# Row sums on one core: the first buffer filled by one load instead of two, and sixteen short reads issued by GpSimd

## The chip, the core and the metric

The kernel runs on one core of a Trainium2 chip. The metric is the device time of the run in microseconds (us). Before the change it is 162.26 us, the median of four runs (162.17 to 162.42).

## What is computed

The input is 32 x 512 rows of 1,024 float32 numbers, 64 MiB; the output is the sum of each row, 16,384 numbers.

```python
def reference(x):                  # x: (32, 512, 1024) float32
    return np.sum(x, axis=-1).astype(np.float32)
```

## The kernel before

The 16,384 rows are spread over 128 partitions, 128 rows on each. `BLOCKS` cuts these 128 into two blocks of 112 and 16 rows per partition; within a block a partition holds rows that follow each other in memory. A block is worked in buffers of `G` = 16 rows per partition, 8,192 KB each: seven for the first block and one for the second. Three such buffers exist (`xpool`, `bufs=3`), so the load into a buffer waits until the reduce of the buffer three before it is done.

All loads are issued by SyncE (`nc.sync.dma_start`, L81, and L95 and L98 for the last buffer). The first buffer is filled by two loads, row 0 of each partition (512 KB) and rows 1 to 15 (7,680 KB); `parts` in L79 says so. The others of the first block take one load each. The last buffer is loaded in five pieces of falling size (9, 4 and 2 rows, then 544 and 480 columns of the last row), so that little work is left behind the last byte.

VectorE sums most rows with one `tensor_reduce` per buffer (L43). ScalarE takes 7 rows of the seventh buffer and some of the last, with an activation that accumulates (L51). The last rows go through a paired add on VectorE (L59), with a one-column copy (L112) between two of them. ScalarE issues the first block's output (L89), SyncE the second's (L114), which is the last transfer.

The order around the change comes from three places. A tile framework puts instructions on each engine's queue in the order in which the program names them, and adds the semaphore waits that the data need. At the very end SyncE waits for every semaphore of the kernel. And after compilation L124 to L143 move the first `EARLY` = 2 instructions of SyncE's body, which are the two loads of the first buffer, ahead of the barrier with which the kernel starts:

```python
loads = [i for i in code if i.engine == sp][:EARLY]
...
at = next(k for k, i in enumerate(code) if i.engine == sp and i.opcode == "Drain")
code[at:at] = loads
```

GpSimd does nothing but set four constants at the start and take part in the barriers.

Of the kernel before, what the change touches and what calls it, by code (L numbers as in the profile page):

```python
# [1 line left out]

# [4 lines left out]

F32 = mybir.dt.float32
ADD = mybir.AluOpType.add
COPY = mybir.ActivationFunctionType.Copy  # L10
X = mybir.AxisListType.X

BLOCKS = (112, 16)
G = 16
ACT_ROWS = 7
CUT = 544
EARLY = 2


@with_exitstack  # L20
def row_sums(
    ctx: ExitStack,
    tc: tile.TileContext,
    x: bass.AP,
    out: bass.AP,
):
    nc = tc.nc
    P = nc.NUM_PARTITIONS

    x_flat = x.flatten_outer_dims()  # L30
    R, D = x_flat.shape
    C = R // P
    assert R % P == 0 and sum(BLOCKS) == C
    out_flat = out.rearrange("a (b c) -> (a b c)", c=1)

    xpool = ctx.enter_context(tc.tile_pool(name="x", bufs=3))
    rpool = ctx.enter_context(tc.tile_pool(name="res", bufs=1))
    part = rpool.tile([P, 1], F32, name="part")
    seen = rpool.tile([P, 1], F32, name="seen")
    pairs = [rpool.tile([P, D // 2], F32, name=f"pairs{i}") for i in range(3)]  # L40

    def rows_dve(xt, res, j, n, c):
        nc.vector.tensor_reduce(  # L43
            out=res[:, c : c + n],
            in_=xt[:, j * D : (j + n) * D].rearrange("p (j d) -> p j d", d=D),
            axis=X,
            op=ADD,
        )

    def sum_act(v, acc):  # L50
        nc.scalar.activation(out=v, in_=v, func=COPY, accum_out=acc)  # L51

    def rows_act(xt, res, j, n, c):
        for i in range(n):
            sum_act(xt[:, (j + i) * D : (j + i + 1) * D], res[:, c + i : c + i + 1])

    def pairs_dve(xt, a, b, first, acc, pairs):
        h = (a + b) // 2
        nc.vector.tensor_tensor_reduce(  # L59
            out=pairs[:, 0 : h - a], in0=xt[:, a:h], in1=xt[:, h:b], scale=1.0, scalar=first,  # L60
            op0=ADD, op1=ADD, accum_out=acc,
        )

    def block(r0, n):
        x_b = x_flat[r0 : r0 + P * n].rearrange("(p c) d -> p (c d)", p=P)
        out_b = out_flat[r0 : r0 + P * n].rearrange("(p c) -> p c", p=P)
        return x_b, out_b, rpool.tile([P, n], F32, name=f"res{r0}")

    full = C - G
    done = 0  # L70
    for b, n in enumerate(BLOCKS):
        x_b, out_b, res = block(done * P, n)
        final = b == len(BLOCKS) - 1
        whole = n - G if final else n
        c = 0
        while c < whole:
            m = min(G, whole - c)
            xt = xpool.tile([P, G * D], F32, tag="xt", name="xt")
            parts = (0, 1, m) if done + c == 0 else (0, m)  # L79
            for i, k in zip(parts, parts[1:]):  # L80
                nc.sync.dma_start(  # L81
                    out=xt[:, i * D : k * D], in_=x_b[:, (c + i) * D : (c + k) * D]
                )
            a = ACT_ROWS if done + c + m == full else 0
            rows_dve(xt, res, 0, m - a, c)
            rows_act(xt, res, m - a, a, c + m - a)
            c += m
        if not final:
            nc.scalar.dma_start(out=out_b, in_=res)  # L89
        done += n  # L90

    xt = xpool.tile([P, G * D], F32, tag="xt", name="xt")
    cuts = [0, 9, 13, 15]
    for i, k in zip(cuts, cuts[1:]):
        nc.sync.dma_start(out=xt[:, i * D : k * D], in_=x_b[:, (c + i) * D : (c + k) * D])  # L95
    last = 15 * D
    for i, k in ((0, CUT), (CUT, D)):
        nc.sync.dma_start(  # L98
            out=xt[:, last + i : last + k],
            in_=x_b[:, c * D + last + i : c * D + last + k],  # L100
        )

    for i, k in zip(cuts[:2], cuts[1:3]):
        h = (k - i) // 2
        rows_dve(xt, res, i, h, c + i)
        rows_act(xt, res, i + h, k - i - h, c + i + h)
    pairs_dve(xt, 13 * D, 14 * D, 0.0, res[:, c + 13 : c + 14], pairs[2])
    rows_act(xt, res, 14, 1, c + 14)
    pairs_dve(xt, last, last + CUT, 0.0, part, pairs[0])


    nc.vector.tensor_copy(out=seen, in_=part)  # L112
    pairs_dve(xt, last + CUT, last + D, part, res[:, c + 15 : c + 16], pairs[1])
    nc.sync.dma_start(out=out_b, in_=res)  # L114


def kernel(tc: tile.TileContext, x: bass.AP, out: bass.AP):
    row_sums(tc, x, out)
    tc.close()
    tc.compile()  # L120

    sp = mybir.EngineType.SP  # L124
    fn = tc.nc.m.functions[0]
    entry, body = None, None
    for blk in fn.blocks:
        ops = [i for i in blk.instructions if i.engine == sp]
        if entry is None:
            entry = blk  # L130
        elif any(i.opcode == "DMACopy" for i in ops):
            body = blk
            break
    code = list(body.instructions)
    loads = [i for i in code if i.engine == sp][:EARLY]
    for load in loads:
        assert load.opcode == "DMACopy" and not load.sync_info.on_wait
        code.remove(load)
    body.instructions = code
    code = list(entry.instructions)  # L140
    at = next(k for k, i in enumerate(code) if i.engine == sp and i.opcode == "Drain")
    code[at:at] = loads
    entry.instructions = code  # L143

# [1 line left out]
_INS = ['x']  # L146
_OUTS = [((32, 512), 'float32')]


# [23 lines left out]
```

## Time and profile before

| what | value |
|---|---|
| median of four runs | 162.26 us |
| the profiled execution's own time | 162.35 us |
| its span, first to last instruction | 160.6 us |
| reduce of a whole buffer (L43, 128x16384) | 17.22 us |
| starts of the first four reduces | 21.84, 41.12, 60.47, 79.82 us |
| HBM read over the span | 67.11 MB, 418 GB/s with what is written |
| from issue to landing: load of 512 KB | 3.6 us |
| from issue to landing: load of 7,680 KB | 21.3 us |
| from issue to landing: output from ScalarE's queue, 56 KB | 7.5 us |
| from issue to landing: output from SyncE's queue, 8 KB | 1.4 us |

The page gives for each engine the time in which it computed; issuing a transfer is not counted as busy. DMA queues are listed by packets: a packet is one contiguous row moved by one of the core's 16 DMA engines, or the four bytes with which an engine reports its share of a transfer as done. q1 is SyncE's queue and q10 ScalarE's. A row of the waits says which engine waited, at which line, for what, and then the us in total, the number of times and the longest. In a table of stretches, a packet is counted where it starts, so short stretches can show a DMA share over 1.

### The profile page before, as it was taken

To read this page: it belongs to the slowest core of one execution; us is meant where nothing else is said; L and a number is where in the kernel's file an instruction comes from. 1 tells how busy PE (TensorE), PEld (TensorE's weight loads), DVE (VectorE), ACT (ScalarE), POOL (GpSimd) and SP (SyncE) were. 2 spreads that over 40 slices of the span, in tenths; PEclk is the share of its full clock that TensorE was granted. 3 is DMA by queue.
4 is the path that set the end of the run, shared out by engine and by line. 5 is a ranking of instruction groups with operands and counts; after the bars stand their busy time and mean duration, and the time that the engine had idled before them with its cause. 6 is when DMAs were issued, how large, how long until landed. Compare 5 with 4: busy or idle time off the path is not lost.

```text
span 160.6 us, 119 instructions
## 1 busy us (share of the span) xinstructions
DVE 121.5 (76%) x16; ACT 17.2 (11%) x31; POOL 0.2 (0%) x4
## 2 busy tenths in 40 slices
DVE  0000059997799959999499994999949998697884
ACT  0000000000000000000000000000000000695892
POOL 0000000000000000000000000000000000000000
DMA  9997998997997996996996996996996997998991
GB/s 376 490 429 306 490 522 359 424 522 310 473 522 310 473 522 261 522 522 261 522 522 261 522 522 261 522 522 261 522 506 278 522 473 310 441 432 364 436 389 44
DMA packets 2160, 67.18 MB, mean 418 GB/s; under 512 B 496, under 2 KB 624, under 8 KB 880
## 3 DMA queue, kind: packets, MB, share of 16 engines
q1 hardware_dynamic: 2016, 67.12, 97.3%
q10 hardware_dynamic: 144, 0.06, 0.1%
HBM read 67.11 MB, written 0.07 MB: 418 GB/s over the span
## 4 chain that ended last, share of the span: by engine, by line
DMA 75%; DVE 23%; SPq 0%; issue 0%; DVEq 0%
DMA xt<-in_x_dram 75%; DVE res L43 21%; DVE pairs L59 1%; SPq L95 0%; DVE seen L112 0%; DVE part L59 0%; DVEq L120 0%; DVE res L59 0%
## 5 line engine op out<-in xcount | busy, mean ns | idle before, releaser
L43 DVE TENSOR_REDUCE res<-xt 128x16 f32<-128x16384 f32 (+3 forms) x9 | 119.8, 13308 | 36.5 <-DMA xt<-in_x_dram 36.5
L51 ACT ACT_TABLE_LOAD x1 | 1.3, 1283 | 138.0 <-DMA xt<-in_x_dram 138.0
L51 ACT ACTIVATE xt<-xt 128x1024 f32<-128x1024 f32 x15 | 15.6, 1043 | 2.5 <-DMA xt<-in_x_dram 2.3
L51 ACT ACTIVATION_READ_ACCUMULATOR xt<-xt 128x1 f32 x15 | 2.8, 186 | 0.0
L59 DVE CUSTOM_DVE_ANT_0 pairs<-xt 128x512 f32<-128x512 f32 (+1 forms) x2 | 1.1, 566 | 0.2 <-DMA xt<-in_x_dram 0.2
L59 DVE CUSTOM_DVE_ANT_0 pairs<-xt,part 128x240 f32<-128x240 f32 x1 | 0.5, 467 | 0.0
L112 DVE COPY seen<-part 128x1 f32<-128x1 f32 x1 | 0.2, 153 | 0.0
L59 DVE DVE_READ_ACCUMULATOR2_ANT res<- 128x1 f32 x2 | 0.2, 80 | 0.0
L157 POOL MEMSET const-bfloat16-1.0<- 128x1 bf16 x1 | 0.1, 101 | 0.0
L157 POOL MEMSET const-uint8-127<- 128x1 uint8 x1 | 0.1, 101 | 0.0
L157 POOL MEMSET const-float32-0.0<- 128x1 f32 x1 | 0.1, 98 | 0.2 <-issue 0.2
L157 POOL MEMSET const-float32-1.0<- 128x1 f32 x1 | 0.1, 98 | 0.0
L59 DVE DVE_READ_ACCUMULATOR2_ANT part<- 128x1 f32 x1 | 0.1, 81 | 0.0
## 6 DMA issues: line engine op xcount, KB each, us to landing
xt<-in_x_dram SPq DMA_DIRECT2D x1, 7680.0 KB, 21.3
xt<-in_x_dram SPq DMA_DIRECT2D x1, 4608.0 KB, 32.5
xt<-in_x_dram SPq DMA_DIRECT2D x1, 2048.0 KB, 37.1
xt<-in_x_dram SPq DMA_DIRECT2D x1, 1024.0 KB, 39.2
xt<-in_x_dram SPq DMA_DIRECT2D x1, 512.0 KB, 3.6
xt<-in_x_dram SPq DMA_DIRECT2D x1, 272.0 KB, 39.4
xt<-in_x_dram SPq DMA_DIRECT2D x1, 240.0 KB, 39.5
xt<-in_x_dram SPq DMA_DIRECT2D x6, 40.8
```

The source lines that it names most:

```text
L43: nc.vector.tensor_reduce(out=res[:, c : c + n], in_=xt[:, j * D : (j + n) * D].rearrange("p (j d) -> p j d", d=D), axis=X, op=ADD,)
L51: nc.scalar.activation(out=v, in_=v, func=COPY, accum_out=acc)
L59: nc.vector.tensor_tensor_reduce(out=pairs[:, 0 : h - a], in0=xt[:, a:h], in1=xt[:, h:b], scale=1.0, scalar=first, op0=ADD, op1=ADD, accum ...
L112: nc.vector.tensor_copy(out=seen, in_=part)
L157: nc = _bacc.Bacc("TRN2", target_bir_lowering=False, num_devices=1)
```

## The change

The first buffer is filled by one load of 16 rows per partition, and `EARLY` becomes 1, so that this one load is again what stands ahead of the barrier. After the loop over the first block's buffers a scratch tile `tag` of 128 x 1,280 numbers is added. VectorE copies the first 16 sums of each partition into it, one every 80 columns. Then GpSimd issues sixteen reads, each from the start of one of the first sixteen rows of `x` into partition 0 of the tile, 17 to 79 numbers long (68 to 316 bytes). Each overwrites an element that the copy has written, so the reads wait for the copy, and the copy waits for the first buffer's reduce. In the new program's order the copy stands on VectorE directly behind the first reduce and ahead of the second. The reads use eight semaphores in turn. Nothing reads the tile afterwards; the wait at the end of the kernel includes the reads.

```diff
-EARLY = 2
+EARLY = 1
...
-            parts = (0, 1, m) if done + c == 0 else (0, m)
-            for i, k in zip(parts, parts[1:]):
-                nc.sync.dma_start(
-                    out=xt[:, i * D : k * D], in_=x_b[:, (c + i) * D : (c + k) * D]
-                )
+            nc.sync.dma_start(out=xt[:, 0 : m * D], in_=x_b[:, c * D : (c + m) * D])
...
+        if done == 0:
+            lengths = (17, 19, 23, 29, 31, 37, 41, 43, 47, 53, 59, 61, 67, 71, 73, 79)
+            tag = rpool.tile([P, 16 * 80], F32, name="tag")
+            nc.vector.tensor_copy(
+                out=tag.rearrange("p (i n) -> p i n", n=80)[:, :, 0], in_=res[:, 0:16]
+            )
+            for i, k in enumerate(lengths):
+                nc.gpsimd.dma_start(
+                    out=tag[0:1, i * 80 : i * 80 + k], in_=x_flat[i : i + 1, 0:k]
+                )
```

## The prediction

> **What bounds the kernel now.** I read the head of the page first, then its DMA queues, then what VectorE and SyncE's queue wait for, then a table of stretches cut where the reduces start, and last the chain.
>
> From the page: the span, the busy engines, and the queues (packets, MB, and the time of their packets as a share of 16 engines' span).
>
> ```profile
> span 160.6 us, 119 instructions
> ...
> DVE 121.5 (76%) x16; ACT 17.2 (11%) x31; POOL 0.2 (0%) x4
> ...
> q1 hardware_dynamic: 2016, 67.12, 97.3%
> q10 hardware_dynamic: 144, 0.06, 0.1%
> ```
>
> VectorE, the busiest engine, has 24% to spare; SyncE's queue q1, which carries all loads, has 2.7%. The 2016 packets are 14 transfers (13 loads, one output) of 128 rows and 16 completions each: 14 x 144 = 2016. So a whole buffer of 8,192 KB is 128 packets of 64 KB, 8 on each of the 16 DMA engines, and every transfer adds one 4-byte completion per engine. q10, one output of 128 rows, shows it alone: 128 + 16 = 144.
>
> Then the waits of VectorE, and those of SyncE's queue (us in total, times, longest):
>
> ```profile
> DVE res L43 <- DMA xt<-in_x_dram: 36.5, 9, 21.8
> ```
>
> ```profile
> SPq L81 <- DVE res L43: 68.9, 4, 17.3
> ...
> SPq L81 <- DMA xt<-in_x_dram: 24.6, 4, 19.5
> ```
>
> VectorE waits for the loads in every stage. SyncE waits 68.9 us for reduces before it may refill a buffer, which looks bad, but a refill is issued with more than a whole buffer still queued: the reduce of the first buffer ends at 21.84 + 17.22 = 39.06 us, when the second has not landed (41.12) and the third is still to move. The stretches (length; VectorE, ScalarE, GpSimd busy; clock; DMA share; GB/s) say whether the loads ever run dry:
>
> ```profile
> 1.00:2.60 1.60, 0.00 (x0) 0.00 (x0) 0.00 (x0) 1.00 0.94 297
> ...
> 21.84:41.12 19.28, 17.22 (x1) 0.00 (x0) 0.00 (x0) 1.00 1.00 435
> 41.12:60.47 19.35, 17.22 (x1) 0.00 (x0) 0.00 (x0) 1.00 1.00 434
> 60.47:79.82 19.35, 17.22 (x1) 0.00 (x0) 0.00 (x0) 1.00 1.00 434
> ...
> 158.90:159.50 0.60, 0.00 (x0) 0.00 (x0) 0.00 (x0) 1.00 0.15 14
> ```
>
> They don't: each stage lasts 19.35 us at a DMA share of 1.00, and the reduce in it 17.22, so VectorE has 2.13 us of slack per stage and the 16 engines have none. Only the beginning is below rate (297 GB/s against 434). The chain by time shows the loads again, and how the end hangs on the last of them (start, us, what):
>
> ```profile
> 58.37 40.78 DMA xt<-in_x_dram
> ...
> 117.28 39.18 DMA xt<-in_x_dram
> 156.46 0.02 issue
> 156.48 0.69 DVE pairs L59
> ```
>
> The reduces in that chain are only the releasers of refills with slack behind them. **So whatever takes time on a DMA engine is paid in full, and what happens on VectorE, GpSimd or SyncE before 137 us is free up to about 2 us a stage.**
>
> One thing more, from the trace's packet records. The 16 completions of one load do not come together: the last engine is 0.67 us behind the first at the end of the first load (2.60 to 3.27 us), 0.63 us at 40 us, 0.53 us at the last load, and the second last stays 0.34 to 0.41 behind. The last at 3.27 us is an engine whose first 4 KB packet took 874 ns; all engines have equal bytes, so a late one has nothing to catch up with. A landing is that of the slowest engine.
>
> **The change, part by part.** The sums are made on the profiled execution, 162.35 us, which is 160.6 of span and 1.75 around it; it lies 0.09 above the median of the four runs, 162.26. I take the 1.75 as fixed and add the difference to the median.
>
> *One load for the first buffer.* The 512 KB load (4 KB rows) and the 7,680 KB load (60 KB rows) become one of 64 KB rows. From the start of one packet to the start of the next on its engine the packet records give 155 ns for 4 KB, 2,264 for 60 KB, 2,415 for 64 KB (medians; 6 for a completion). Per row 155 + 2,264 - 2,415 = 4 ns go, 8 rows per engine: 0.03 us, and one completion of 0.006. Together **-0.04 us** on every engine.
>
> The ramp is a separate matter. The 16 packets that start first took 369 ns on average; later 4 KB packets take 159. In 1.00 to 2.60 us the engines moved 297 of 434 GB/s. Had the engine that starts last, at 1.46 us, moved its eight packets at 155 ns, it and all others would have been done at 2.70 us, not 3.27. So at best a single load brings the landings 0.57 us forward. At worst it adds as much as the slowest 60 KB packet just behind the ramp did, 2,629 - 2,267 = +0.36. A cold start stays a cold start whatever the row's length, so I take 0 and keep both ends.
>
> *EARLY from 2 to 1.* SyncE still issues the first load ahead of the barrier. The second and third buffers follow from 1.2 us on, as before, with 20 us of the first load still to move. 0, hidden by that load; it would cost only if the issue slipped behind 20 us.
>
> *The copy into the scratch tile.* In the program's order it stands on VectorE between the first and second reduce and waits for the first. A 128x1 copy (L112) took 0.15 us; call this one 0.2. It runs from 39.06 us inside the idle 2.06 us ahead of 41.12. Queued behind it is the second reduce, which waits for its load anyway. 0; without that idle time it would be 0.2. No later wait of a load passes through the copy: the refills wait on reduces. The Trainium skill's page "SBUF — State Buffer" ("SBUF: two separate sides", the box on the "DVE blocks DMA" trap) would have GpSimd locked out from writing descriptors beside a two-port VectorE operation; by it the reads would only come later, and the sum would not move, since nothing but the kernel's last wait asks for them.
>
> *Sixteen reads from GpSimd.* No row of before shows a transfer from this queue. GpSimd is idle after 0.4 us, so issuing is free. The second eight reads each wait for one of the first eight (eight semaphores in turn); behind them on GpSimd is only the end of the kernel, 100 us away. What counts is the DMA engines' time. Each read brings one row of 68 to 316 bytes and, as every transfer in this trace, 16 completions: 16 x 17 = 272 packets, 17 per engine if the rows spread evenly. Nearest rows: a completion among loads takes 6 ns to the next packet, a row of 448 B on q10 21, one of 64 B in the last output 7. (The stretch 158.90 to 159.50 gives a check from above: 0.15 x 0.60 us x 16 engines = 1.44 us for the last output's 144 packets, 10 ns each.) So 16 completions are 0.10 us per engine, and the row, between 7 and 21 ns, 0.02. If only the engine that carries the row completes, the 0.10 falls to 0.01.
>
> Does the short row hold up the stream behind it? For: it is a cold read of HBM from another queue. Against: in 151 to 154 us the rows of q10 stand between 16 KB load packets and cost nothing beyond their 21 ns, but they are read from SBUF. The only cold reads here are the 16 first packets of the kernel: 369 - 159 = 0.21 us more on average, 874 - 159 = 0.72 at most. Ends 0 and 0.72; I take the mean, 0.21, once per engine, since a cold HBM read is the nearer row.
>
> A rule speaks against the reads more strongly: the Trainium skill's page "DMA: Bandwidth & Descriptors" ("Anatomy of one DMA — SWDGE (gpsimd) path") gives such a transfer a fixed 2.0 us, nearly all of it waiting for the write's receipt. On the path that would be 16 x 2.0 = 32 us as an estimate; it would be latency of transfers that nobody waits for, and here it counts for nothing.
>
> *The end.* SyncE's last waits now include eight more semaphores, those of the reads. The instruction records show these waits stepping 0.06 us apart (159.70, 159.76, 159.83, 159.88). The new program has four more wait instructions; three of them, by its order, stand ahead of the wait for the output, which left SyncE 0.92 us idle (158.78 to 159.70), and one behind it: **+0.06 us**.
>
> Sum: -0.04 + 0.10 + 0.02 + 0.21 + 0.06 = **+0.35 us**, to 162.26 + 0.35 = 162.6.
>
> **Rivals.**
>
> *The reads hide entirely but for their packets* (not slower): the engines read ahead over a change of queue as they do over rows. Sum without the 0.21: +0.14, 162.4; with one completion per read +0.05, 162.3. For it speaks q10 among the loads. Both are within 0.2% (0.32 us), about what a measurement of this kernel can tell from no change.
>
> *The first load starts better* (faster): the slowest engine of the ramp sets all later landings, and fewer, longer first packets may not produce it. With the reads hidden, +0.14 - 0.57 = -0.43, 161.8. It decides once the ramp gives back more than 0.14 + 0.32 = 0.46 us. Against it: 16 cold starts will still have a slowest one, and the second last engine was only 0.27 us earlier.
>
> *Every packet of the new queue stalls its engine*, not the row alone: 17 x 0.21 = 3.6 us at the bound, so between the forecast and 162.4 + 3.6 = 166.0. Against it q10; for it, that no row shows this queue.
>
> *The reads don't fall where the title puts them.* The copy could hold them to the end and the last wait would catch them; the order and 39 us against 160 exclude it.
>
> **How the numbers follow.** Forecast 162.6, chance 0.48; reads hidden, 0.20; better start, 0.17; every packet stalls, 0.15. The forecast's +0.35 is barely over the 0.32, so 0.08 of its 0.48 count as within. Slower by over 0.2%: 0.40 + 0.15 = 0.55; within: 0.08 + 0.20 = 0.28; faster: 0.17. Range: the packets with the best ramp, +0.14 - 0.57 = -0.43, give 161.8; with the worst ramp and the longest cold read, 0.14 + 0.36 + 0.72 = +1.22, 163.5. It leaves out most of the last rival, under 2 in 10.
>
> **What would show it.** q1 with 13 x 144 = 1872 packets and a new queue with 272 (32 if one engine completes). The first reduce within 0.1 us of 21.84 if the ramp stays. The stages of 19.35 us unchanged, but for 0.3 us more, in sum, in the one or two that end near 60.5 and 79.8. The copy within the idle time ahead of the second reduce. 0.06 us more from the output's landing to the end. I am wrong if a stage without reads grows, if the first landing moves by over 0.3 us, or if the time outside the span changes from 1.75.

## The result and the profile after

The changed kernel takes 162.65 us (median of 43 runs, 162.43 to 163.07) against 162.18 us for the kernel before (64 runs). The ratio is 1.0022, 95% interval 1.0016 to 1.0028: slower by 0.22%, 0.36 us by the ratio and 0.47 us between the medians. Forecast were +0.35 us and 162.6 us. The profiled execution took 162.70 us with a span of 160.9, so the time around the span has not changed noticeably (1.8 against 1.75).

The page after, its head and its queues:

```profile
span 160.9 us, 138 instructions
...
DVE 121.7 (76%) x17; ACT 17.2 (11%) x31; POOL 8.5 (5%) x20
...
q1 hardware_dynamic: 1872, 67.12, 96.9%
q0 software_dynamic: 512, 0.00, 0.2%
q10 hardware_dynamic: 144, 0.06, 0.1%
```

q1 has lost the 144 packets of one load, as worked out. The new queue q0 carries 512 packets, not 272: 32 for each read instead of 17.

The groups of the reads and of the copy (busy, mean ns, then the idle time ahead of them):

```profile
L91 POOL DMA_DIRECT2D tag<-in_x_dram x16 | 8.3, 526 | 72.1 <-DVE tag L87 39.2
...
L87 DVE COPY tag<-res 128x16 f32<-128x16 f32 x1 | 0.2, 181 | 0.0
```

The copy takes 0.18 us, and VectorE still waits 1.90 us for the second buffer after it: it is hidden. Issuing a read costs GpSimd 0.53 us; it waits 39.2 us for the copy and, in total, 32.8 us for earlier reads, and nobody waits for GpSimd.

The stretches after, cut where the reduces start:

```profile
1.00:2.60 1.60, 0.00 (x0) 0.00 (x0) 0.00 (x0) 1.00 1.80 614
21.94:41.28 19.34, 17.40 (x3) 0.00 (x0) 1.60 (x3) 1.00 1.00 434
41.28:60.66 19.38, 17.22 (x1) 0.00 (x0) 4.15 (x9) 1.00 1.00 433
60.66:80.24 19.58, 17.22 (x1) 0.00 (x0) 2.07 (x4) 1.00 0.99 428
80.24:99.48 19.24, 17.22 (x1) 0.00 (x0) 0.52 (x1) 1.00 1.01 436
99.48:118.88 19.40, 17.22 (x1) 0.00 (x0) 0.00 (x0) 1.00 1.00 432
```

The first row is not a fast start. A packet is counted where it starts, and fifteen of the sixteen first 64 KB packets start in these 1.6 us (the other a little earlier); that the sixteen take 3.08 us on average and later ones 2.42 is seen only in the packet records. The first reduce starts 0.10 us later than before (21.94), the fourth 0.42 (80.24), the fifth 0.30 (99.48): the delay grows a little in stages that hold reads, and it was there before the first of them. The end of the chain:

```profile
117.58 39.06 DMA xt<-in_x_dram
156.65 0.03 issue
156.67 0.69 DVE pairs L59
```

The last rows' work starts at 156.67 instead of 156.48, 0.19 us later in this one execution; the last output is issued 0.22 us later (158.48), and from there to the last instruction the instruction records show 2.45 us instead of 2.31, 0.14 more. Together 0.36.

So the sum fitted. The experiments ask whether its terms did.

### The profile page after: what moved, and what is told of

Its sections match the earlier page's. It is cut to its first block, busy times and chain, and to the rows that moved or that the text cites. A ratio compares the mean times of both kernels' runs of the same rounds, so it can differ in the third digit from the quotient of the medians.

```text
span 160.9 us, 138 instructions
## 1 busy us (share of the span) xinstructions
DVE 121.7 (76%) x17; ACT 17.2 (11%) x31; POOL 8.5 (5%) x20
## 4 chain that ended last, share of the span: by engine, by line
DMA 75%; DVE 22%; SPq 0%; issue 0%; DVEq 0%
DMA xt<-in_x_dram 75%; DVE res L43 21%; DVE pairs L59 1%; SPq L101 0%; DVE seen L118 0%; DVE part L59 0%; DVEq L126 0%; DVE res L59 0%
## 5 line engine op out<-in xcount | busy, mean ns | idle before, releaser
L91 POOL DMA_DIRECT2D tag<-in_x_dram x16 | 8.3, 526 | 72.1 <-DVE tag L87 39.2
```

Source lines behind the costliest of these rows:

```text
L91: nc.gpsimd.dma_start(out=tag[0:1, i * 80 : i * 80 + k], in_=x_flat[i : i + 1, 0:k])
```

## The experiments

The kernel before was run beside each (162.16 to 162.19 us, medians). Times are medians; ratios are to the kernel before.

**The two halves of the change.** `merge_only` is the changed kernel without the copy and the reads, so it has the single first load alone. `reads_only` is the kernel before with the copy and the reads alone.

> One load for the first buffer, no copy and no reads. As predicted (the ramp does not care how long the first rows are): 0.04 us faster than before, first reduce within 0.05 of before's start, end unchanged. Theory from the trace after (the first 64 KB packet of an engine loses 0.66 us on average, where the split start loses 0.41 over its packets): +0.25 - 0.04 = 0.2 us slower, ratio about 1.0013, first reduce near 21.95 us, end unchanged. Rival (the whole change lies in the first load): 0.4 us slower.

Measured, `merge_only`: 162.51 us, ratio 1.0019 (1.0010 to 1.0028).

> The split first load of before, with the copy and the sixteen reads. As predicted: 0.10 + 0.02 + 0.21 + 0.06 = 0.39 us slower, 0.21 of it from cold rows. Theory from the trace after: 32 small packets per engine at 6 ns, 0.19 us, nothing for the rows, and 0.14 us at the end behind the output: 0.33 us slower, ratio about 1.002, 512 packets on the new queue. Rival (all in the first load): within 0.05 us of before.

Measured, `reads_only`: 162.36 us, ratio 1.0018 (1.0008 to 1.0029); medians 0.17 us apart, 0.29 by the ratio. The interval, 0.13 to 0.47 us, holds the theory's 0.33 and the prediction's 0.39 alike, so the time does not choose between them; the packet records further down do.

Each half costs something. By the medians their sum (0.32 + 0.17 = 0.49 us) is what the whole costs (0.47); by the ratios it is 0.31 + 0.29 = 0.60 against 0.36, so how exactly they add up is not settled by these runs. The prediction's -0.04 us for the single load, with nothing for its ramp, is refuted, and so is the rival that puts the whole change there. In merge_only all stages have their old length and the loss is there at the first reduce (start, us, then in brackets the wait ahead of it):

```profile
22.04 17.22 DVE L43 TENSOR_REDUCE res<-xt 128x16 f32<-128x16384 f32 x1 [22.04 <-DMA xt<-in_x_dram]
41.36 17.22 DVE L43 TENSOR_REDUCE res<-xt 128x16 f32<-128x16384 f32 x1 [2.10 <-DMA xt<-in_x_dram]
60.70 17.22 DVE L43 TENSOR_REDUCE res<-xt 128x16 f32<-128x16384 f32 x1 [2.12 <-DMA xt<-in_x_dram]
```

The first reduce starts 0.20 us later than before's 21.84, and the stages last 19.32 and 19.34 us: a loss of the start.

**One read instead of sixteen.**

```diff
-lengths = (17, 19, 23, 29, 31, 37, 41, 43, 47, 53, 59, 61, 67, 71, 73, 79)
+lengths = (17,)
```

> As the one before, but a single read of 17 numbers. Theory from the trace after: 32 packets in all, 0.01 us per engine, and an end that grows by less than 0.1 us since one semaphore is added and not eight: 0.05 us slower. Rival (using GpSimd's queue at all has a fixed price): as slow as with sixteen reads, 0.3 us. As predicted, with one cold row on one engine: 0 to 0.2 us.

Measured, `one_read`: 162.30 us, ratio 1.0010 (1.0001 to 1.0019). The interval reaches from nothing to 0.3 us and decides little alone. Its profile does, at the end: from SyncE's last arrival at the barrier to the last instruction there are 0.75 us, as with sixteen reads (0.75) and in the changed kernel (0.76), against 0.68 before and 0.67 with the single load alone. GpSimd's drain (94 to 107 ns against 70 to 75) and its clearing of the semaphores (136 to 138 against 93) last longer once its queue has been used. That is a fixed price of about 0.08 us. The queue of this kernel:

```profile
q1 hardware_dynamic: 2016, 67.12, 97.2%
q10 hardware_dynamic: 144, 0.06, 0.1%
q0 software_dynamic: 32, 0.00, 0.0%
```

32 packets for one read of 68 bytes, two per engine: in the records one engine moves the row and a completion, and each of the other fifteen two packets of 4 bytes.

**How long the first rows are.** Four kernels without reads cut the first buffer elsewhere; a fifth, with the single load, changes the spacing of the partitions.

```diff
-            parts = (0, 1, m) if done + c == 0 else (0, m)
+            parts = (0, 4, m) if done + c == 0 else (0, m)           # first_16k; (0, 2, m) in first_8k
...
+            cuts = (0, 256, m * D) if done + c == 0 else (0, m * D)  # first_1k, in columns; (0, 16, m * D) in first_64b
```

> No copy and no reads; the first buffer in two loads of 4 and 12 rows, so the first packets are of 16 KB. Theory (the ramp loses more the longer the first packets are; 4 KB lost 0.41 us, 64 KB 0.66): between before and the single load, about 0.1 us slower. As predicted (length does not matter): within 0.05 us of before. Rival (what matters is that there are two loads, not their cut): as before, too, so the first landing and the packets of the ramp decide between these two.

Measured, `first_16k`: 162.26 us, ratio 1.0008 (0.9999 to 1.0016). By the time it can't be told from before; its profile has a later start (table below).

> No copy and no reads; the first buffer in two loads, the first 256 columns of each partition (1 KB rows) and the rest. Theory (the ramp loses more the longer the first packets are): the mean completion of the whole first buffer up to 0.1 us earlier than before's 20.95, the run 0 to 0.1 us faster than before. Rival (what matters is that a packet of some KB opens each engine; below that the engines only run dry until the second load is issued 0.4 us later): mean completion near 21.2 as with the single load, 0.1 to 0.3 us slower than before.

Measured, `first_1k`: 162.67 us, ratio 1.0033 (1.0020 to 1.0046). The theory had it faster and fails; the rival has the direction, but the loss is larger than its 0.1 to 0.3 us.

> As the one before with 16 columns (64-byte rows). If short first packets alone make the ramp better: mean completion of the first buffer at or below 20.95, the run no slower than before. If the engines need bytes to move while the second load is being issued: the eight rows are done in 0.1 us and the engines wait 0.3 to 0.4 us; mean completion 21.2 to 21.4, 0.2 to 0.4 us slower.

Measured, `first_64b`: 162.86 us, ratio 1.0041 (1.0027 to 1.0054). Slower, and by more than the second theory had.

> No copy and no reads; the first buffer in loads of 2 and 14 rows, first packets of 8 KB. Mean completion of the first buffer so far: 21.79 us with 64 B, 21.36 with 1 KB, 20.96 with 4 KB, 21.16 with 16 KB, 21.2 with 64 KB. If 4 KB is near the best: between 20.96 and 21.16, the run 0 to 0.15 us slower than before. If the best lies between 4 and 16 KB: under 20.9, and 0.1 us faster than before.

Measured, `first_8k`: 162.18 us, ratio 0.9997 (0.9988 to 1.0005): no difference from the 4 KB of before.

A landing depends on the luck of the slowest engine, so the mean over the 16 engines of the time at which they report the whole first buffer, called mean completion here, is the steadier number (packet records, one profile each; the 4 KB row is seven profiles, all kernels here with that cut):

| first rows | the 16 packets that start first, ns (range or mean) | mean completion, us | time against before |
|---|---|---|---|
| 64 B | 8 to 11 | 21.79 | +0.70 |
| 1 KB | 44 to 60 | 21.36 | +0.51 |
| 4 KB (before) | 322 to 463 (before 369) | 20.94 to 20.99 | 0 |
| 8 KB | 549 | 20.94 | +0.02 |
| 16 KB | 1168 | 21.16 | +0.07 |
| 64 KB (single load) | 3129 (merge_only), 3081 (after) | 21.21, 21.18 | +0.32 |

The means and the times agree within 0.15 us. For 16 KB that is not enough to decide: the mean is 0.21 us late, the time 0.07 (0.13 by the ratio, between nothing and 0.26), and the profiled execution took 162.50 us, 0.24 above the median of its kernel. What 16 KB rows cost is not settled.

"Shorter is better" falls at the lower end. With 64 bytes the engines are done by 1.24 us, and the first packets of the second load start at 1.48 us, because SyncE issues it 0.43 us behind the first; and those large packets are then as slow (2.4 to 3.4 us where 2.41 is normal) as if nothing had been moved before them. So two things cost here: a gap until the second load (0.61 us per engine on average with 64 B, 0.07 with 1 KB) and a slow first large packet (3.13 and 3.05 us). 4 and 8 KB rows escape both. The first reduce of first_8k is the earliest of all (start, us, and the wait ahead of it in brackets):

```profile
21.57 17.22 DVE L43 TENSOR_REDUCE res<-xt 128x16 f32<-128x16384 f32 x1 [21.57 <-DMA xt<-in_x_dram]
40.85 17.22 DVE L43 TENSOR_REDUCE res<-xt 128x16 f32<-128x16384 f32 x1 [2.05 <-DMA xt<-in_x_dram]
```

Its 0.27 us over before is the slowest engine alone: the means are 20.94 and 20.95, and the runs did not keep it.

With `EARLY` = 1 SyncE also issues the second buffer's load sooner, at 0.77 us in merge_only where before has 1.24. No run has the single load in the old order. But first_64b issues that load at 1.26 us and its first large packets are as slow as those of merge_only, so the sooner issue isn't needed for a slow first packet.

```diff
-BLOCKS = (112, 16)
+BLOCKS = (111, 17)
...
-            a = ACT_ROWS if done + c + m == full else 0
+            a = ACT_ROWS if done + c + m == full - 1 else 0   # ScalarE's 7 rows, in the buffer of 15
```

> The single first load, with blocks of 111 and 17 rows per partition instead of 112 and 16, so that partitions lie 444 KB apart instead of 448 KB, which is 7 times 64 KB; the later buffers change with it (one of 15 rows, one of 1), so only the first load is to be read. If the 16 engines' first packets are slow because they start at like places in HBM: first 64 KB packets near 2.8 us instead of 3.1, mean completion of the first buffer near 20.9. If a cold start with 64 KB packets is slow by itself: unchanged, 3.1 us and 21.2.

Measured, `stride_444k`: first packets 3,154 ns, mean completion 21.23 us, as with 448 KB (the time of this one run, 165.01 us, holds the other buffers and is not read). A like place of the sixteen rows in HBM, as far as this spacing changes it, is not the reason. Against their steady length the packets of the first load lose, per engine, 0.36 us in sum with 4 KB rows (before), 0.43 with 8 KB, 0.60 with 16 KB, and 0.66 (after) or 0.71 (merge_only) in the first 64 KB packet alone. Not every engine's first packet is slow: the one that starts last took 2.43 us in merge_only and 2.42 in the changed kernel, though 3.28 with 444 KB. Why the loss grows with the row stays open.

**Where a read's bytes go.** The changed kernel's rows are too short to show which engine carries them, so the reads were made 4 KB long.

```diff
+            lengths = (1021,) * 16    # long_1021, into partition 0; (1024,) * 16 in long_1024
...
+                p = i % 8 * 4 + i // 8 * 64    # spread_1021: p = 0, 4, ... 28, 64, 68, ... 92; 1024 in spread_1024
+                nc.gpsimd.dma_start(out=tag[p : p + 1, 0:1021], in_=x_flat[i : i + 1, 0:1021])
```

> The split first load of before and sixteen reads from GpSimd, each of 1,021 numbers (4,084 bytes, into two places in turn). Theory from the trace after (all sixteen rows go through one and the same DMA engine, and only an engine that is ahead of the others can hide them): 16 x 155 ns = 2.5 us on that engine, about 0.3 us of it hidden by its lead over the last engine, 2.2 us on the landings: 164.4 us. If the rows are spread over the 16 engines, as the prediction had them: 0.155 + 0.19 us per engine and the end, 162.6 us. Rival (a row stalls its engine as a cold read, 0.2 us each, beside its own time): over 165.5 us.

Measured, `long_1021`: 164.43 us, ratio 1.0141 (1.0127 to 1.0155), where the theory had 164.4 and the others 162.6 and over 165.5.

> The same with 1,024 numbers, which the compiler cuts into 16 rows of 256 bytes. Theory (sixteen rows of a read go to sixteen engines): per read and engine one row at about 14 ns and one or two completions at 6, 0.3 us in all, and 0.1 us at the end: 162.5 to 162.7 us, 2 us below the run with 1,021 though it moves more bytes. Rival (the bytes of the reads decide, not the engine that moves them): as slow as with 1,021.

Measured, `long_1024`: 165.12 us, ratio 1.0184 (1.0170 to 1.0198). The theory fails: the rows do go to sixteen engines (256 packets of 256 bytes, 18 ns each), and it is slower still. Its stages:

```profile
41.07:60.75 19.68, 17.22 (x1) 0.00 (x0) 1.46 (x3) 1.00 0.99 427
60.75:81.15 20.40, 17.22 (x2) 0.00 (x0) 1.95 (x4) 1.00 0.96 412
81.15:101.54 20.39, 17.22 (x2) 0.00 (x0) 1.95 (x4) 1.00 1.07 461
101.54:121.46 19.92, 17.22 (x1) 0.00 (x0) 1.46 (x3) 1.00 0.98 422
121.46:140.81 19.35, 17.22 (x1) 0.00 (x0) 0.00 (x0) 1.00 0.96 416
```

Every stage with reads in it is longer, one without is not. In the completions a single engine falls behind, 2.5 us after all others by 120 us; its own 64 KB packets take up to 2,665 ns while fifteen others write into partition 0. 64 KB at the pace of one engine (65,536 bytes in 2,415 ns) are 2.4 us, as if the way into partition 0 were full. The next two runs write each read into another partition: `spread_1024` with 1,024 numbers, `spread_1021` with 1,021.

> The same with 1,024 numbers, cut into sixteen rows of 256 bytes each. If the place of writing decides (64 KB into one partition is as much as its engine moves of the loads in 2.4 us): no engine falls behind, 0.3 to 0.5 us slower than before, 162.5 to 162.7 us. If 256-byte rows are dear in themselves wherever they land: 165 us as before.

Measured, `spread_1024`: 162.94 us, ratio 1.0049 (1.0037 to 1.0061). With the same rows written to sixteen places the laggard is gone (the last engine 0.02 us behind the second last at 118 us):

```profile
41.01:60.61 19.60, 17.22 (x1) 0.00 (x0) 3.87 (x9) 1.00 0.99 429
60.61:80.12 19.51, 17.22 (x1) 0.00 (x0) 1.94 (x4) 1.00 1.00 431
80.12:99.61 19.49, 17.22 (x1) 0.00 (x0) 0.48 (x1) 1.00 1.01 431
```

That is 2.2 us less than into one partition. It is 0.2 to 0.4 us above the expectation. The 64 KB packets between 44 and 119 us took 0.35 us per engine more in sum than at their usual 2,418 ns, which I had not counted; but the profiles without reads have 0.05 to 0.2 us of that in the same stretch, so it explains the difference in part only.

> The sixteen reads of 1,021 numbers, now each into another partition (0, 4, ... 28, 64, ... 92). Open so far: the run with 1,024 numbers moved its rows evenly over sixteen engines and yet one engine fell 2.5 us behind, so it may be the place of writing (partition 0) that is shared. If the engine that carries the rows decides: the rows still go one by one through one engine, 16 x 155 ns, 164.4 us as in the run into partition 0. If the place of writing decides and the carrying engine is that of the place: 0.155 + 0.19 us per engine, 162.5 to 162.7 us.

Measured, `spread_1021`: 164.80 us, ratio 1.0159 (1.0145 to 1.0172).

```profile
60.81 17.22 DVE L43 TENSOR_REDUCE res<-xt 128x16 f32<-128x16384 f32 x1 [2.60 <-DMA xt<-in_x_dram]
81.09 17.22 DVE L43 TENSOR_REDUCE res<-xt 128x16 f32<-128x16384 f32 x1 [3.07 <-DMA xt<-in_x_dram]
101.42 17.22 DVE L43 TENSOR_REDUCE res<-xt 128x16 f32<-128x16384 f32 x1 [3.11 <-DMA xt<-in_x_dram]
```

Spreading the places does not help where the row is not cut: VectorE waits 3.07 us for a load where before has 2.13, and one engine is 2.0 us behind the others at 120 us. The rows follow each other 4.99 us apart or little more (2.6 where a load ends), which is one and the same engine's time for two 64 KB packets (4.83) and a row (0.155). So both hold, the carrying engine and the place, and either alone costs over 2 us for 64 KB.

The Trainium skill's page "DMA: Bandwidth & Descriptors" ("Why a DMA increments its semaphore by 16 and not by 1") has the number of engines chosen as the largest one up to 16 that divides the outer size of the access pattern. That makes one for 1,021 numbers, a prime, and sixteen for a row of 1,024 that is cut in sixteen, and the runs agree. It also has a GpSimd transfer on fewer than sixteen engines start at a cursor that goes round them; here the rows of all sixteen reads stayed on one engine, and the records decide.

## Why the prediction was right, step by step

The forecast time held, and the direction. That the sum held is luck: four of its terms were mis-sized (the ramp, the completions, the cold read and the end), and they made up for each other.

- **Single load, packets (-0.04 us):** not to be seen by itself; it lies inside what the start lost.
- **Single load, ramp (0, bounds -0.57 to +0.36):** this step failed. "A cold start stays a cold start whatever the row's length, so I take 0" is refuted: the mean completion of the first buffer moved from 20.95 to 21.2 us, and the single load alone costs 0.32 us. The value was inside the bounds and near the upper one, which came from the 60 KB packets behind the ramp. The rival with a better start had the sign wrong.
- **EARLY and the copy (0):** right as far as the traces show. The first packets start at 1.00 us before and after, and the copy ran from 39.19 us into the idle time ahead of 41.28.
- **Completions of the reads (0.10 us):** half of what they are. The 6 ns per packet held, but a read has two packets per engine, not one: 32 x 6 = 0.19 us. From the completion of the first buffer to that of the sixth, at 118 us, the changed kernel took 96.82 us on the mean of the engines, merge_only 96.66, 0.16 us less. That difference alone shows little: the profile of before, without reads, took 96.82, too, because its sixth load took 19.44 us on that mean, where the four before took 19.33 to 19.36. The 0.19 us stands on the reads' own packets.
- **Rows (0.02 us, spread evenly):** wrong in place. All sixteen go through one engine, where they take 193 ns in sum by the records; each other engine has a 4-byte packet in their place, 96 ns in sum. What hides this is that the engine was the first of all to report the first buffer, 0.74 us ahead of the slowest, and still 0.68 ahead at the sixth.
- **Cold read (0.21 us):** refuted. From the start of a row to the next packet on its engine there are 8 ns for 68 bytes to 17 for 316; the engine does not wait. That the latency of the reads would count for nothing was right: it was 8.8 us and more, over the 2.0 us that the prediction quotes, and nothing but the end of the kernel waited for it. The rival in which every packet stalls falls with it. The rival in which the reads hide but for their packets was right about the mechanism.
- **The end (+0.06 us):** the added wait is there (four steps instead of three behind the output's release, 0.06 us), and GpSimd's longer drain and clearing, 0.08, were not seen ahead.

In the forecast's terms: 0.24 (the start, with the packets) + 0.19 + 0.00 + 0.14 = 0.57 us, where the runs have 0.36 to 0.47. What is left, 0.1 to 0.2 us, is not settled; in the profiles the slowest engine of a start is up to 0.25 us sooner or later from one execution to the next, and kernels with the same start differ by that.

None of the three signs named for a wrong prediction came, though terms were wrong: the first landing moved by 0.10 us (0.20 in merge_only), not by over 0.3, the time outside the span stayed, and the last stage without reads kept its length (118.88 to 138.24 us). The signs named for a right one show more: the new queue has 512 packets and not 272, and the first reduce moved by just the 0.1 us that was allowed for an unchanged ramp. Nor did the reads stay within the stages that end near 60.5 and 79.8 us. From issue to landing they took:

```profile
DMA to landing us min/median/max: 8.8/33.7/36.7
```

Each engine takes one packet of the new queue per 64 KB packet, so a read needs two rounds, 4.84 us (2.44 where a load ends), and the last one ended at 113.6 us.

## What to carry to other kernels

In a kernel whose DMA engines are busy throughout, price a small transfer by the packets it puts on each engine and by the engine and partition that its bytes share, not by its bytes alone or its latency. Check a sum that fits by undoing its parts: here a start that was thought free and a cold read that was thought dear were wrong by about the same amount. In this kernel the first transfer did best with rows of 4 and 8 KB: long enough to keep the engines at work until the second is issued, and short enough that no 64 KB packet opens the stream. For 16 KB the runs do not decide.

## What was not expected of the hardware

- A first packet of 64 KB took 3.1 us on average against 2.42 later, on nearly all engines, and equally so behind a first load of 64-byte rows.
- Sixteen single-row reads from GpSimd's queue all used one DMA engine, and each read put 32 packets on the engines, 31 of them of 4 bytes.
- 64 KB written into one partition by sixteen engines made one engine 2.5 us late; written into sixteen partitions, none.
- Having used GpSimd's queue once made the end of the kernel 0.08 us longer.
- A short read beside a stream of 64 KB packets was served one packet per 2.42 us and engine. The eighth of eight reads issued together landed some 37 us after its issue.
